# A hybrid decoder block: four pairs of SwiGLU tiles by seven products of quarters

## The chip, the cores and the metric

The kernel runs on one core of one Trainium2 chip. The metric is the device time of one execution in microseconds, median of the runs shown; lower is better.

## The reference, cut to what matters

One decoder block on 512 positions of width 1024, all in float32: two token mixers side by side, merged by gates, then a SwiGLU channel mixer of inner width 2816.

```python
h = rmsnorm(x, norm1_g)
z_glu, z_rx, z_rg, z_ga, z_gb = jnp.split(h @ w_in + b_in, split_idx, axis=-1)

u = z_glu[..., :D_CONV] * jax.nn.sigmoid(z_glu[..., D_CONV:])
u = silu(layernorm(causal_depthwise_conv(u, conv_dw_w, conv_dw_b), ...))
y_a = u @ conv_w_out + conv_b_out

xb = causal_depthwise_conv(z_rx, lru_conv_w, lru_conv_b)
y_b = (rg_lru(xb, ...) * gelu(z_rg)) @ lru_w_out

x = x + (sigmoid(z_ga) * y_a + sigmoid(z_gb) * y_b) @ w_mix_out
h = rmsnorm(x, norm2_g)
x = x + (silu(h @ ffn_w1) * (h @ ffn_w3)) @ ffn_w2
return rmsnorm(x, norm_f_g)
```

The change is in the last matrix products but one, `h @ ffn_w1` and `h @ ffn_w3`: 1024 inputs, 2 x 2816 outputs, 512 positions.

## The kernel before

**Numbers in two parts.** Every float32 operand of a product is split into a high part of TensorE's reduced float32 type (a cast, by ACT) and the low remainder (a subtraction, by DVE or POOL: `split_to`, L106). A product of two split operands is three matmuls: high by high, high by low, low by high (`mm3`, L354). One output tile of 128 columns with 1024 inputs is 8 x 3 = 24 matmuls with 512 positions as the moving side.

**Weights come in chunks.** A chunk is 128x1024 floats, 0.5 MB. `wchunk` (L121) only lists it; `emit_chunk` (L124) issues its load into one of four `raw` buffers (SP's queue), the cast into one of five `hl` buffers, and the subtraction; the `raw` buffer is free when the subtraction has read it, the `hl` buffer when PE has used it. `weights` (L150) emits up to four chunks ahead of the one that is wanted. In the input stage POOL subtracts, from the next stage on DVE.

**Stages in PE's order.** The input stage (`ORDER`, L190; tiles named z, and the gates g) with the depthwise convolution on DVE beside it (`beside`); yb, ya, the mixing product (mxr), the turn of the normalised rows into `h2p` (th), the SwiGLU tiles (f) and the output product (or). The SwiGLU tiles go in pairs k and k + 11, for k = 0 to 10: four products of 24 matmuls, `f1_k`, `f3_k`, `f1_{k+11}`, `f3_{k+11}`. Pair 0 (`first_two`) is done on half a sequence (256 columns) at a time, since the second half of `h2p` comes later.

**Seven products instead of eight.** The mixing and output products already use the Strassen-Winograd scheme: a product of 2 x 2 blocks by seven block products and some sums (`Sevenfold`, L727). Its sums of activations are made in `pair` (L742), its sums of weights in `make_sums` (L265): a load of two blocks into two `raw` buffers, four DVE operations, four stores to DRAM (tiles named ows and ot), from where they are later loaded as chunks. For the output product `make_sums` is called once after each pair of SwiGLU tiles, by `ffn_out` (L875).

**Who sets the order.** Most instructions are put in the order of their engine by a scheduler that works from the order in which they are written and its own estimate of their lengths; each engine then runs its list in order, and SP's list of DMA issues too. `issue_after(ins)` puts a block's instructions of the same engine behind `ins`. Tiles named long, short, raw and hl come from pools with a fixed number of buffers: a new tile waits until an old one is released.

Of the kernel before, what the change touches and what calls it, by code (L numbers as in the profile page):

```python
# [26 lines left out]
ND = D // P  # L27
NR = DR // P
NF = DF // P


SLOTS, SHORT = 69, 5
RAW = 4
HL = 5
AHEAD = 4
# [2 lines left out]
FEW, MANY = 32, 112  # L38

LAG = 12  # L40


ROWS = [
# [32 lines left out]
def tile_block(ctx, tc, a, out):  # L76
    nc = tc.nc
    pool = lambda name, bufs, **k: ctx.enter_context(tc.tile_pool(name=name, bufs=bufs, **k))
    consts = pool("consts", 1)
    raws = pool("raws", RAW)  # L80
    hls = pool("hls", HL)
    psum = pool("psum", 6, space=bass.MemoryType.PSUM)
    psum2 = pool("psum2", 2, space=bass.MemoryType.PSUM)

    def tiles(tag, bufs):
        p_ = pool(tag, bufs)
        return lambda name, dtype=F32: p_.tile([P, T], dtype, tag=tag, name=name)
# [12 lines left out]

    vec, act, pe, pool_e = nc.vector, nc.scalar, nc.tensor, nc.gpsimd

    def sub(eng, o, x, y):
        eng.tensor_tensor(out=o, in0=x, in1=y, op=ALU.subtract)  # L104

    def split_to(h, l, full, eng, copy=act.copy):  # L106

        copy(h, full)  # L108
        sub(eng, l, full, h.bitcast(F32))
# [9 lines left out]
    emitted = [0]  # L119

    def wchunk(key, src, kt, cols, where="hl", lo=pool_e, after=None):  # L121
        chunks.append((key, src, kt, cols, where, lo, after))

    def emit_chunk():  # L124
        key, src, kt, cols, where, lo, after = chunks[emitted[0]]
        emitted[0] += 1
        n = kt * cols
        raw = raws.tile([P, 1024], F32, tag="raw", name=f"raw_{key}")
        rv = raw[:, :n]
        if callable(src):  # L130
            src(raw)
        else:
            nc.sync.dma_start(rv.rearrange("p (k n) -> p k n", k=kt), src)  # L133
# [78 lines left out]
    dram = ctx.enter_context(tc.tile_pool(name="dram", bufs=1, space=bass.MemoryType.DRAM))  # L212
# [70 lines left out]
    ff_order = [j for k in range(NF // 2) for j in (k, k + NF // 2)]  # L283
    for j in ff_order:
        wchunk(f"f1_{j}", w1[:, :, j * P : (j + 1) * P], ND, P, lo=vec)
        wchunk(f"f3_{j}", w3[:, :, j * P : (j + 1) * P], ND, P, lo=vec)
# [67 lines left out]
    def mm3(ps, ws, xs, lo_last=False):  # L354


        n = 3 * len(ws)
        i = 0
        three = [((wh, xh), (wh, xl), (wl, xh)) for (wh, wl), (xh, xl) in zip(ws, xs)]
        if lo_last:  # L360
            three = [q[:2] for q in three] + [q[2:] for q in three]
        for l, r in (q for qs in three for q in qs):
            pe.matmul(ps, l, r, start=i == 0, stop=i == n - 1)  # L363
# [46 lines left out]
    def parts_of(pair_tiles, cs=slice(0, T)):  # L410
        return [(h[:, cs], l[:, cs]) for h, l in pair_tiles]
# [9 lines left out]
    HALVES = [slice(0, 256), slice(256, 512)]  # L421
    EARLY = 2
# [42 lines left out]
    ab, e, s, s2, po, c4 = (sm[:, i, :] for i in range(6))  # L465
# [44 lines left out]
    def beside():  # L510
# [63 lines left out]
    def run_beside(n):  # L574
        for _ in range(n):
            next(side, None)
# [49 lines left out]
    hs = xb  # L626
# [49 lines left out]
    y = []  # L676

    def rg(j):
# [2 lines left out]
        vec.tensor_tensor(out=ps, in0=hs[j], in1=ps, op=ALU.mult)  # L681
        y.append(split(f"y{j}", ps, vec))

    for kind, j in ORDER:
        if kind == "u":
            glu(j)
        elif kind == "rx":
            rx(j)
            run_beside(4)
        elif kind == "g":  # L690
            gates(j)
        elif kind == "r":
            recur(j)
        elif kind == "rg":
            rg(j)
            run_beside(6)
        elif kind == "gb":
            sig(GB, j, sgb, "sgb")
            run_beside(6)
        else:  # L700
            sig(GA, j, sga, "sga")
            run_beside(8)


    for j in range(8):
        ws = w_tiles(f"lo{j}_0", 5) + w_tiles(f"lo{j}_1", 5)
        ps = bank(f"yb{j}")
        mm3(ps, ws, y)
        vec.tensor_tensor(out=sgb[j], in0=ps, in1=sgb[j], op=ALU.mult)
        run_beside(8)  # L710
        if j in (2, 4, 6):
            mixq.make_sums(j // 2 - 1)
    yb = sgb
    run_beside(1000)


    add = lambda o, x, y: vec.tensor_tensor(out=o, in0=x, in1=y, op=ALU.add)
    LO, HI = HALVES
# [8 lines left out]
    class Sevenfold:  # L727
# [28 lines left out]
        def product(self, banks, i, x_, w_, start, stop, again=False):  # L756

            (xh, xl), (wh, wl) = x_, w_
            ts = slice(i * P, (i + 1) * P)
            for n, (l_, r_) in enumerate(((xh, wh), (xh, wl), (xl, wh))):  # L760
                pe.matmul(banks[i], l_[:, ts], r_, start=start and n == 0, stop=stop and n == 2, skip_group_check=again)  # L761
# [66 lines left out]
    h2p = [pairt(f"h2{c}") for c in range(ND)]  # L828
# [42 lines left out]


    o7 = Sevenfold(outq)

    def ffn_out(j, p1, p3):  # L875
        s_ = shortt(f"si{j}")
        act.activation(s_, p1, AF.Silu)
        o7.tile(j, lambda cs, dst: vec.tensor_tensor(out=dst, in0=s_[:, cs], in1=p3[:, cs], op=ALU.mult))  # L878
        if j >= NF // 2:
            with tc.issue_after(turned):  # L880
                outq.make_sums(j - NF // 2)

    first_two = ff_order[:EARLY]
# [13 lines left out]
    for j in ff_order[EARLY:]:  # L897
        p1, p3 = bank(f"f1_{j}"), bank(f"f3_{j}")
        mm3(p1, w_tiles(f"f1_{j}", ND), h2)
        mm3(p3, w_tiles(f"f3_{j}", ND), h2)  # L900
        ffn_out(j, p1, p3)


    x2 = [[longt(f"x2b{t}{h}") for h in range(2)] for t in range(NT)]
# [93 lines left out]
```

## Time and profile before

| | |
|---|---|
| runs | 819.69, 819.13, 818.77 us; median 819.13 |
| profiled execution | 819.27 us, span of its instructions 817.5 us |
| mean granted clock of TensorE | 0.997 |
| PE busy | 805.6 us, 99% |
| DVE busy | 607.6 us, 74% |
| ACT busy | 420.0 us, 51% |
| POOL busy | 149.7 us, 18% |
| moved by DMA | 130.31 MB |

The profile is of one execution. Engines: PE multiplies, PEld loads its weights, DVE, ACT and POOL work on tiles, SP issues DMAs. A row of a group gives line, engine, operation, out<-in by the program's names, shapes and count, then busy time and mean ns of one, then the engine's idle time before them and who ended it. A row of the chain or the timeline begins with its start and length in us. A row of waits reads: engine and line that waited, for whom, us in total, times, longest.

### The profile page before, as it was taken

The numbers are of one execution on the slowest core, as the hardware profiler recorded it, in microseconds if no ns is written. First come the engines' busy times: TensorE is split into PE (matmuls) and PEld (weight loads), VectorE is DVE, ScalarE is ACT, GpSimd is POOL, SyncE is SP. The second block draws the span as 40 slices with busy tenths as digits, with TensorE's granted clock in tenths as the row PEclk, the third lists the DMA queues.
The fourth block names the chain that finished last, engine by engine and source line by source line (L and its number), as shares of the span: only waits on it lengthen the run. The fifth ranks groups of instructions, "written<-read, shape, count | busy, mean of one in ns | idle before, by whom it ended". The sixth has DMA issues, their size and how long they took to land.

```text
span 817.5 us, 10585 instructions
## 1 busy us (share of the span) xinstructions
PE 805.6 (99%) x3750; PEld 673.7 (82%) x3750; DVE 607.6 (74%) x954; ACT 420.0 (51%) x587; POOL 149.7 (18%) x84
## 2 busy tenths in 40 slices
PE   8999999999999999999999999999999999999996
PEld 7988888888888888888888998888888888888885
DVE  4699999999989976876968866455555444688556
ACT  7546688778678565743336543222222222476443
POOL 3564456535534530000000000000000000000000
PEclk9999999999999999999999999999999999999998
DMA  6634433444323412369538448656665666876552
GB/s 207 168 97 117 122 92 102 111 108 112 101 85 110 132 49 67 114 196 292 169 126 248 148 134 267 190 178 204 193 181 187 198 194 205 263 265 205 171 165 103
DMA packets 158343, 130.31 MB, mean 159 GB/s; under 512 B 11367, under 2 KB 128531, under 8 KB 158291
## 3 DMA queue, kind: packets, MB, share of 16 engines
q1 hardware_dynamic: 158291, 129.65, 52.1%
q8 instruction: 29, 0.48, 0.2%
q14 instruction: 23, 0.19, 0.1%
HBM read 108.78 MB, written 17.83 MB: 155 GB/s over the span
## 4 chain that ended last, share of the span: by engine, by line
PE 96%; DMA 1%; SPq 1%; DVE 0%; POOL 0%; ACT 0%; issue 0%
PE z L363 34%; PE f L363 29%; PE or L761 13%; PE yb L363 7%; PE ya L363 5%; PE mxr L761 5%; PE g L643 3%; DMA raw_in<-in_w_in_dram 1%; SPq L319 1%; PE th L403 0%; SPq L312 0%; POOL hl_in L104 0%; DVE of L921 0%; ACT hl_in L108 0%; SPq L133 0%
## 5 line engine op out<-in xcount | busy, mean ns | idle before, releaser
L522 DVE SCALAR_TENSOR_TENSOR cv<-u,par,cv 128x511 f32<-128x511 f32 (+17 forms) x240 | 162.6, 728 | 1.4 <-ACT cv L519 1.2
L104 POOL TENSOR_TENSOR hl_in<-raw_in,hl_in 128x1024 fp32r<-128x1024 f32 x52 | 125.6, 2419 | 136.6 <-ACT hl_in L108 131.8
L108 ACT CAST hl_f<-raw_f 128x1024 fp32r<-128x1024 f32 x44 | 46.2, 1053 | 143.5 <-PE f L363 81.1
L104 DVE TENSOR_TENSOR hl_f<-raw_f,hl_f 128x1024 fp32r<-128x1024 f32 x44 | 53.8, 1222 | 37.4 <-ACT hl_f L108 37.3
L108 ACT CAST hl_in<-raw_in 128x1024 fp32r<-128x1024 f32 x52 | 54.2, 1043 | 11.3 <-PE z L363 7.1
L878 DVE TENSOR_TENSOR ou<-si,f 128x256 f32<-128x256 f32 x22 | 9.3, 422 | 62.2 <-PE f L363 61.6
L108 ACT CAST hl_ob<-raw_ob 128x1024 fp32r<-128x1024 f32 (+1 forms) x23 | 23.4, 1016 | 42.4 <-PE or L761 19.3
L363 PE MATMUL z<-h10h,hl_in 128*128 128x512 f32 (+1 forms) x112 | 42.3, 379 | 1.2 <-DVE h10l L407 0.9
L104 DVE TENSOR_TENSOR hl_ob<-raw_ob,hl_ob 128x1024 fp32r<-128x1024 f32 (+1 forms) x23 | 27.0, 1176 | 19.7 <-ACT hl_ob L108 19.5
L363 PE MATMUL z<-h14h,hl_in 128*128 128x512 f32 (+1 forms) x112 | 41.7, 374 | 0.0
L363 PE MATMUL z<-h13h,hl_in 128*128 128x512 f32 (+1 forms) x112 | 41.7, 374 | 0.0
L363 PE MATMUL z<-h15h,hl_in 128*128 128x512 f32 (+1 forms) x112 | 41.7, 374 | 0.0
L363 PE MATMUL z<-h16h,hl_in 128*128 128x512 f32 (+1 forms) x112 | 41.7, 374 | 0.0
L363 PE MATMUL z<-h11h,hl_in 128*128 128x512 f32 (+1 forms) x112 | 41.7, 374 | 0.0
L363 PE MATMUL z<-h17h,hl_in 128*128 128x512 f32 (+1 forms) x112 | 41.7, 374 | 0.0
L363 PE MATMUL z<-h12h,hl_in 128*128 128x512 f32 (+1 forms) x112 | 41.7, 374 | 0.0
L363 PE MATMUL f<-h22h,hl_f 128*128 128x512 f32 (+1 forms) x96 | 35.4, 371 | 0.0
L363 PE MATMUL f<-h23h,hl_f 128*128 128x512 f32 (+1 forms) x96 | 35.4, 372 | 0.0
L363 PE MATMUL f<-h25h,hl_f 128*128 128x512 f32 (+1 forms) x96 | 35.4, 372 | 0.0
L363 PE MATMUL f<-h24h,hl_f 128*128 128x512 f32 (+1 forms) x96 | 35.4, 371 | 0.0
L363 PE MATMUL f<-h26h,hl_f 128*128 128x512 f32 (+1 forms) x96 | 35.4, 371 | 0.0
L363 PE MATMUL f<-h20h,hl_f 128*128 128x512 f32 (+1 forms) x96 | 35.0, 373 | 0.3 <-ACT h20h L406 0.3
(812 smaller groups left out, 2258.0 us busy)
## 6 DMA issues: line engine op xcount, KB each, us to landing
raw_in<-in_w_in_dram SPq DMA_DIRECT2D x52, 512.0 KB
raw_f<-in_ffn_w_dram SPq DMA_DIRECT2D x44, 512.0 KB
ows<-in_ffn_w_dram SPq DMA_DIRECT2D x22, 512.0 KB
ot<-ows SPq DMA_DIRECT2D x44, 256.0 KB
raw_ob<-in_ffn_w_dram SPq DMA_DIRECT2D x33, 256.0 KB
raw_ot<-ot SPq DMA_DIRECT2D x33, 256.0 KB
raw_lo<-in_lru_w_out_dram SPq DMA_DIRECT2D x16, 320.0 KB
x<-in_x_dram SPq DMA_DIRECT2D x16, 256.0 KB
```

What stands on the lines that cost most here:

```text
L104: eng.tensor_tensor(out=o, in0=x, in1=y, op=ALU.subtract)
L108: copy(h, full)
L319: nc.sync.dma_start(xt[t][h], x_nat[:, t, h * T : (h + 1) * T])
L363: pe.matmul(ps, l, r, start=i == 0, stop=i == n - 1)
L522: vec.scalar_tensor_tensor(out=acc[c][:, s:], in0=u[c][:, : T - s], scalar=dw(c, s), in1=acc[c][:, s:], op0=ALU.mult, op1=ALU.add)
L643: pe.matmul(ps, l, r, start=k == 0, stop=k == len(mms) - 1)
L761: pe.matmul(banks[i], l_[:, ts], r_, start=start and n == 0, stop=stop and n == 2, skip_group_check=again)
L878: o7.tile(j, lambda cs, dst: vec.tensor_tensor(out=dst, in0=s_[:, cs], in1=p3[:, cs], op=ALU.mult))
```

## The change

Pairs 2, 3, 4 and 5 (`SEVEN`) of the SwiGLU tiles are done by seven products of quarters; the other seven pairs stay as they were.

* For such a pair the weight of each of w1 and w3 is cut in 2 x 2 blocks: upper and lower half of the 1024 inputs, columns of tile k and of tile k + 11. The activations are cut in upper and lower half of the inputs and first and second half of the positions. A block product is 4 x 3 matmuls for w1 and as many for w3, of 256 columns, into the two halves of one PSUM bank (`product`): 24 matmuls of 256 columns from one chunk. There are seven, in the order b11, b21, b22, t2, t1, t3, t4. r1 is added to in place by t2 and by t4; ACT copies it out between (`c11`, `q`). Five DVE additions put the results together, four SiLUs of 256 columns and four multiplications follow.
* The four sums of weights t1 to t4 of each of the four pairs are made in the input stage (`make_f_sums`): 16 items, each of four loads of 128x256 (128 KB) into one of two `wsums` buffers, four operations on POOL, placed behind the newest weight subtraction there, and four stores to DRAM; one item every third step of `ORDER`. 64 loads and 64 stores are added to SP's queue there, 64 operations to POOL's. In the SwiGLU stage a sum is loaded as a chunk.
* The sums of activations are made once, behind the turn of `h2p` (`f_inputs`): eight additions on POOL (128x512), sixteen DVE operations of 128x256, eight splits of 128x512 on ACT and DVE.
* `make_sums` for the output product moves from "after each pair" to: two after pair 1, none after pairs 2 and 4, one after 3 and 5, two after each of 6, 7 and 8, the last one after 9 (`out_sums`).
* The long buffers go from 69 to 65, to make room for `wsums`.

In PE's list nothing changes ahead of pair 2. In the lists of ACT and DVE two neighbours are swapped in the input stage; the rest of what differs lies behind pair 0.

```diff
-SLOTS, SHORT = 69, 5
+SLOTS, SHORT = 65, 5
+SEVEN = (2, 3, 4, 5)
+SUMS_AT, SUMS_STEP, SUMS_LAG, STORE_LAG = 4, 3, 2, 5
...
+    wsums = pool("wsums", 2)
...
+    def make_f_sums():
+        todo = [(k, i, c) for k in SEVEN for i in range(2) for c in (0, 2)]
+        sums_due, stores_due = [], []
+        n = 0
+        while todo or sums_due or stores_due:
+            if stores_due and emitted[0] >= stores_due[0][0]:
+                stores_due.pop(0)[1]()
+            if sums_due and n >= sums_due[0][0]:
+                sums_due.pop(0)[1]()
+            if todo and n >= SUMS_AT and (n - SUMS_AT) % SUMS_STEP == 0:
+                k, i, c = todo.pop(0)
+                raw = wsums.tile([P, 1024], F32, tag="wsum", name=f"fws{k}_{i}_{c}")
+                q = [raw[:, 256 * m : 256 * m + 256] for m in range(4)]
+                with tc.issue_after(newest["load"]):
+                    for m, v in zip(("b11", "b12", "b21", "b22"), q):
+                        nc.sync.dma_start(v.rearrange("p (k n) -> p k n", k=2), f_quarter(m, k, (w1, w3)[i], c, c + 2))
+                def sums(q=q, k=k, at=T * i + P * c):
+                    q11, q12, q21, q22 = q
+                    with tc.issue_after(newest["sub"]):
+                        sub(pool_e, q22, q22, q12)
+                        sub(pool_e, q12, q12, q11)
+                        pool_e.tensor_tensor(out=q11, in0=q22, in1=q11, op=ALU.add)
+                        sub(pool_e, q21, q21, q11)
+                    def stores():
+                        with tc.issue_after(newest["load"]):
+                            for m, v in (("t1", q12), ("t2", q11), ("t3", q22), ("t4", q21)):
+                                nc.sync.dma_start(f_sums[m, k][:, at : at + 256], v)
...
     for kind, j in ORDER:
+        next(f_sums_steps, None)
...
-        if j >= NF // 2:
-            with tc.issue_after(turned):
-                outq.make_sums(j - NF // 2)
...
+    def f_inputs():
+        for k in range(4):
+            a1, a2 = [longt(f"hf{c}") for c in (k, k + 4)]
+            for v, c in ((a1, k), (a2, k + 4)):
+                pool_e.tensor_tensor(out=v, in0=h2p[c][0].bitcast(F32), in1=h2p[c][1].bitcast(F32), op=ALU.add)
+            g = [longt(f"hs{k}_{i}") for i in range(2)]
+            s1, s2, s3, s4 = (v[:, cs] for v in g for cs in HALVES)
+            add(s1, a1[:, HI], a2[:, HI])
+            sub(vec, s2, s1, a1[:, LO])
+            sub(vec, s3, a1[:, LO], a1[:, HI])
+            sub(vec, s4, a2[:, LO], s2)
+            s12, s34 = [split(f"hs{k}_{i}", v, vec) for i, v in enumerate(g)]
...
+    def ffn_seven(k):
...
+        product(r1, "a11", "b11")
+        act.copy(c11, r1)
+        product(r2, "a12", "b21")
+        add(c11, r2, c11)
+        out_of(c11, u_[:, LO])
+        product(r3, "s4", "b22")
+        product(r1, "s2", "t2", True)
+        act.copy(q, r1)
+        product(r5, "s1", "t1")
+        add(q, r5, q)
+        add(c12, r3, q)
+        out_of(c12, u_[:, HI])
+        product(r7, "s3", "t3")
+        act.copy(c21, r7)
+        add(q, r7, q)
+        out_of(q, v_[:, HI])
+        product(r1, "a22", "t4", True)
+        add(c21, r1, c21)
+        out_of(c21, v_[:, LO])
+        o7.pair(k, u_, v_)
...
+    for k in range(1, KF):
+        if k in SEVEN:
+            ffn_seven(k)
+            out_sums(k % 2)
+            continue
...
+        out_sums(2 if k < KF - 1 else KF)
```

More of the change, by code (lines that the diff above doesn't have):

```diff
@@ L101, in tile_block @@
     vec, act, pe, pool_e = nc.vector, nc.scalar, nc.tensor, nc.gpsimd
+    newest = {}
     def sub(eng, o, x, y):
-        eng.tensor_tensor(out=o, in0=x, in1=y, op=ALU.subtract)
+        return eng.tensor_tensor(out=o, in0=x, in1=y, op=ALU.subtract)
     def split_to(h, l, full, eng, copy=act.copy):
         copy(h, full)
-        sub(eng, l, full, h.bitcast(F32))
+        last = sub(eng, l, full, h.bitcast(F32))
+        if eng is pool_e:
+            newest["sub"] = last.ins
         return h, l
@@ L132, in emit_chunk @@
         else:
-            nc.sync.dma_start(rv.rearrange("p (k n) -> p k n", k=kt), src)
+            newest["load"] = nc.sync.dma_start(rv.rearrange("p (k n) -> p k n", k=kt), src).ins
         if where == "hl":
@@ L282, in tile_block, with f_quarter @@
     w3 = a["ffn_w3"][0].rearrange("(k p) n -> p k n", p=P)
[L283 to L286, printed above, removed]
+    KF = NF // 2
+    f_sums = {(n, k): dram.tile([P, 1024], F32, tag=f"f{n}_{k}", name=f"f{n}_{k}") for k in SEVEN for n in ("t1", "t2", "t3", "t4")}
+    def f_quarter(n, k, w_, c0, c1):
+        c, j = 4 * (int(n[1]) - 1), k + KF * (int(n[2]) - 1)
+        return w_[:, c + c0 : c + c1, j * P : (j + 1) * P]
@@ new lines, in f_chunk, with load @@
+    def f_chunk(n, k):
+        def load(raw_t):
+            if n[0] == "t":
+                nc.sync.dma_start(raw_t, f_sums[n, k][:, :])
+            else:
+                for i, w_ in enumerate((w1, w3)):
+                    nc.sync.dma_start(raw_t[:, i * T : (i + 1) * T].rearrange("p (k n) -> p k n", k=4), f_quarter(n, k, w_, 0, 4))
+        wchunk(f"f{n}_{k}", load, 8, P, lo=vec)
+    def make_f_sums():
[25 more added lines that the diff above has]
+                                nc.sync.dma_start(f_sums[m, k][:, at : at + 256], v)
+                    stores_due.append((emitted[0] + STORE_LAG, stores))
+                sums_due.append((n + SUMS_LAG, sums))
+            n += 1
+            yield
@@ L287, in tile_block @@
+    for k in range(KF):
+        if k in SEVEN:
+            for n in ("b11", "b21", "b22", "t2", "t1", "t3", "t4"):
+                f_chunk(n, k)
+        else:
+            for j in (k, k + KF):
+                wchunk(f"f1_{j}", w1[:, :, j * P : (j + 1) * P], ND, P, lo=vec)
+                wchunk(f"f3_{j}", w3[:, :, j * P : (j + 1) * P], ND, P, lo=vec)
     outq = Quartered("o", a["ffn_w2"][0].rearrange("(k p) n -> p k n", p=P), NF // 2, vec)
@@ L682, in rg @@
         y.append(split(f"y{j}", ps, vec))
+    f_sums_steps = make_f_sums()
     for kind, j in ORDER:
+        next(f_sums_steps, None)
         if kind == "u":
@@ L710, in tile_block @@
         run_beside(8)
+        next(f_sums_steps, None)
         if j in (2, 4, 6):
@@ L714, in tile_block @@
     run_beside(1000)
+    for _ in f_sums_steps:
+        pass
     add = lambda o, x, y: vec.tensor_tensor(out=o, in0=x, in1=y, op=ALU.add)
@@ L873, in tile_block, with out_sums @@
     o7 = Sevenfold(outq)
+    sums_of = iter(range(KF))
+    def out_sums(n):
+        with tc.issue_after(turned):
+            for _ in range(n):
+                k = next(sums_of, None)
+                if k is not None:
+                    outq.make_sums(k)
     def ffn_out(j, p1, p3):
@@ L878, in ffn_out @@
         o7.tile(j, lambda cs, dst: vec.tensor_tensor(out=dst, in0=s_[:, cs], in1=p3[:, cs], op=ALU.mult))
-        if j >= NF // 2:
-            with tc.issue_after(turned):
-                outq.make_sums(j - NF // 2)
-    first_two = ff_order[:EARLY]
+    first_two = [0, KF]
     wf = [(w_tiles(f"f1_{j}", ND, 0), w_tiles(f"f3_{j}", ND, 0)) for j in first_two]
@@ L896, in tile_block @@
         ffn_out(j, *pf[i])
[L897 to L901, printed above, removed]
+    f_in = {n: [] for n in ("a11", "a12", "a22", "s1", "s2", "s3", "s4")}
+    def f_inputs():
[10 more added lines that the diff above has]
+            s12, s34 = [split(f"hs{k}_{i}", v, vec) for i, v in enumerate(g)]
+            for n, p_, cs in (
+                ("a11", h2p[k], LO), ("a12", h2p[k + 4], LO), ("a22", h2p[k + 4], HI),
+                ("s1", s12, LO), ("s2", s12, HI), ("s3", s34, LO), ("s4", s34, HI),
+            ):
+                f_in[n].append(tuple(v[:, cs] for v in p_))
@@ new lines, in tile_block, with product, out_of @@
+    with tc.issue_after(turned):
+        f_inputs()
+    def ffn_seven(k):
+        u_, v_ = longt(f"ou{k}"), longt(f"ov{k}")
+        def product(ps, x_, w_, again=False):
+            h, l = weights(f"f{w_}_{k}")
+            for i in range(2):
+                for c, (xh, xl) in enumerate(f_in[x_]):
+                    for m, (lw, rx_) in enumerate(((h, xh), (h, xl), (l, xh))):
+                        pe.matmul(
+                            ps[:, HALVES[i]], lw[:, 4 * i + c, :], rx_, start=not (again or i or c or m),
+                            stop=bool(i and c == 3 and m == 2), skip_group_check=True,
+                        )
+        def out_of(c, dst):
+            act.activation(c[:, LO], c[:, LO], AF.Silu)
+            vec.tensor_tensor(out=dst, in0=c[:, LO], in1=c[:, HI], op=ALU.mult)
+        r1, r2, r3, r5, r7 = bank(f"fr1_{k}"), bank2(f"fr2_{k}"), bank(f"fr3_{k}"), bank2(f"fr5_{k}"), bank(f"fr7_{k}")
+        product(r1, "a11", "b11")
+        c11 = shortt(f"c11_{k}")
+        act.copy(c11, r1)
[4 more added lines that the diff above has]
+        product(r1, "s2", "t2", True)
+        q = shortt(f"q_{k}")
+        act.copy(q, r1)
+        product(r5, "s1", "t1")
+        add(q, r5, q)
+        c12 = shortt(f"c12_{k}")
+        add(c12, r3, q)
+        out_of(c12, u_[:, HI])
+        product(r7, "s3", "t3")
+        c21 = shortt(f"c21_{k}")
+        act.copy(c21, r7)
[4 more added lines that the diff above has]
+        out_of(c21, v_[:, LO])
+        o7.uv.append((u_, v_))
+        o7.pair(k, u_, v_)
@@ L904, in tile_block @@
+    for k in range(1, KF):
+        if k in SEVEN:
+            ffn_seven(k)
+            out_sums(k % 2)
+            continue
+        for j in (k, k + KF):
+            p1, p3 = bank(f"f1_{j}"), bank(f"f3_{j}")
+            mm3(p1, w_tiles(f"f1_{j}", ND), h2)
+            mm3(p3, w_tiles(f"f3_{j}", ND), h2)
+            ffn_out(j, p1, p3)
+        out_sums(2 if k < KF - 1 else KF)
     x2 = [[longt(f"x2b{t}{h}") for h in range(2)] for t in range(NT)]
```

## The prediction

> **What bounds the kernel now.** I read the head of the page first, then the chain that ended last, then who waited on PE, then stretches of time.
>
> ```profile
> span 817.5 us, 10585 instructions
> PE 805.6 (99%) x3750; PEld 673.7 (82%) x3750; DVE 607.6 (74%) x954; ACT 420.0 (51%) x587; POOL 149.7 (18%) x84
> PE 96%; DMA 1%; SPq 1%; DVE 0%; POOL 0%; ACT 0%; issue 0%
> GB/s 207 168 97 117 122 92 102 111 108 112 101 85 110 132 49 67 114 196 292 169 126 248 148 134 267 190 178 204 193 181 187 198 194 205 263 265 205 171 165 103
> ```
> The end is set by PE: 96% of the chain. The pieces of the chain give what PE pays for one matmul.
>
> ```profile
> 72.14 1.85 PE g L643 x8
> ...
> 246.68 65.30 PE z L363 x288
> ...
> 461.61 11.51 PE f L363 x96
> ...
> 478.61 226.43 PE f L363 x1033
> 705.04 102.97 PE or L761 x453
> ```
> A product of 512 columns costs 65.30 / 288 = 226.7 ns. The 96 matmuls of 11.51 us are the first SwiGLU tiles on half a sequence, 256 columns: 119.9 ns each. So a half costs 13 ns more than half of a whole. Pairs 1 to 10 of SwiGLU tiles end where the "or" products begin, at 705.04; pair 2, the first that is changed, starts nine pairs earlier (below: 21.76 us each), at 509.2.
>
> PE hardly ever waits (all waits of over a few tenths are in the first 27 us):
>
> ```profile
> PE z L363 <- POOL hl_in L104: 0.3, 1, 0.3
> PE f L363 <- ACT h20h L406: 0.3, 1, 0.3
> ```
>
> Stretches (busy us of PE, PEld, DVE, ACT, POOL, then clock, DMA share, GB/s): the input stage, the first halves, pairs 1 and 2, and four later pairs.
>
> ```profile
> 28.00:280.00 252.00, 252.00 (x1156) 210.32 (x1155) 243.20 (x382) 178.53 (x221) 127.01 (x70) 1.00 0.38 105
> 461.00:484.00 23.00, 22.66 (x184) 21.95 (x182) 14.56 (x29) 12.74 (x25) 0.00 (x0) 1.00 0.29 93
> 484.00:528.00 44.00, 44.00 (x210) 37.05 (x209) 27.84 (x42) 13.83 (x19) 0.00 (x0) 1.00 0.76 239
> 528.00:616.00 88.00, 88.00 (x390) 72.89 (x389) 45.42 (x72) 24.10 (x32) 0.00 (x0) 1.00 0.62 192
> ```
> DVE is nearly full in the input stage (243.2 of 252 us) and half empty beside the SwiGLU pairs; POOL works in the input stage alone.
>
> **PE's part of the change.** A pair of tiles is four products of 24 matmuls of 512 columns: 96 x 226.7 ns = 21.76 us. With seven products of quarters it is 7 x 24 = 168 matmuls of 256 columns: 168 x 119.9 ns = 20.14 us. That is 12.5% less arithmetic, but only 1.62 us a pair, since the 13 ns are paid 168 times. Four pairs: 6.5 us, all on the path.
>
> [...]
>
> Could loading weights hold the short matmuls back? In the stretch 461:484, 182 loads took 21.95 us, 121 ns each, beside matmuls of that size; a load fits. I take nothing for it.
>
> **The vector engines beside the pairs.** Rows of DVE, ACT, and POOL (mean ns of one after the comma):
>
> ```profile
> L104 DVE TENSOR_TENSOR hl_f<-raw_f,hl_f 128x1024 fp32r<-128x1024 f32 x28 | 34.2, 1221 | 27.1 <-ACT hl_f L108 27.1
> L104 DVE TENSOR_TENSOR ows<-ows,ows 128x512 f32<-128x512 f32 x16 | 11.0, 688 | 0.3
> L878 DVE TENSOR_TENSOR ou<-si,f 128x256 f32<-128x256 f32 x16 | 6.8, 422 | 50.8 <-PE f L363 50.8
> ```
> ```profile
> L108 ACT CAST hl_f<-raw_f 128x1024 fp32r<-128x1024 f32 x28 | 29.5, 1054 | 110.1 <-PE f L363 65.1 <-issue 45.1
> L877 ACT ACTIVATE si<-f 128x512 f32<-128x512 f32 x16 | 9.4, 588 | 0.0
> L108 ACT CAST os1p<-os 128x256 fp32r<-128x256 f32 x8 | 3.2, 400 | 0.0
> ```
> ```profile
> L104 POOL TENSOR_TENSOR hl_in<-raw_in,hl_in 128x1024 fp32r<-128x1024 f32 x52 | 125.6, 2419 | 136.6 <-ACT hl_in L108 131.8 <-PE g L643 2.9 <-DMA raw_gate<-in_lru_wa_dram 1.4
> L104 POOL TENSOR_TENSOR hl_gate<-raw_gate,hl_gate 128x512 fp32r<-128x512 f32 x10 | 13.4, 1340 | 14.1 <-ACT hl_gate L108 9.8 <-DMA raw_gate<-in_lru_wx_dram 4.2
> L104 POOL TENSOR_TENSOR hl_gate<-raw_gate,hl_gate 32x256 fp32r<-32x256 f32 x6 | 4.9, 820 | 0.5
> ```
> A changed pair asks of DVE: seven chunk subtractions, 7 x 1.22 = 8.5; five additions from PSUM, by the 512-wide row 5 x 0.69 = 3.4; four multiplications, 4 x 0.42 = 1.7; the pair's own sums and split, 0.69 + 5 x 0.42 = 2.8; half a set of the sums for the last weights, 2 x 0.69 = 1.4. That is 17.8 of 20.14 us. ACT: 7 x 1.05 + 3 copies of 0.59 + 4 x 0.40 + 1.0 = 11.7 us. Both fit, DVE with 2.3 us to spare, so in the steady state I charge nothing. What hides it is the ring of five split weights: a chunk's buffer is free four products ahead of its use.
>
> ```profile
> 499.49 1.23 DVE L104 TENSOR_TENSOR hl_f<-raw_f,hl_f 128x1024 fp32r<-128x1024 f32 x1 [0.31 <-ACT hl_f L108]
> ```
> ```profile
> 519.92 0.39 PE L363 MATMUL f<-h20h,hl_f 128*128 128x512 f32 x1
> ```
> This chunk is ready 19.2 us before PE takes it; with products of 24 x 119.9 ns = 2.88 us the ring reaches only 4 x 2.88 = 11.5 us ahead, and cast and subtraction take 2.3 of that.
>
> The entrance is the tight place. The sums of the activations are built once, between 479.6 and the third product of pair 2 (509.2 + 5.8 = 515.0): DVE 16 x 0.42 + 8 x 0.69 = 12.2 us, POOL 8 x 1.34 = 10.7 us, ACT 8 x 0.59 = 4.7 us. Add to the 27.84 us that DVE works in 484:528 these 12.2, three more chunks 3.7, five additions 3.4, and take off one set of sums that now comes later, 2.8: 44.3 of 44 us. So DVE falls behind there, and the order of its queue decides. In the changed order of DVE the first addition of pair 1's sums stands ahead of the last activation split, and it waits for a load into a buffer that the stores of pair 0's sums must leave first. The t4 chunk's load waits likewise for the stores of pair 1's sums, and on SP the loads of pair 3 are queued behind it. Rows of a load and its landing, and of waits for stores:
>
> ```profile
> 482.57 3.22 SPq L133 DMA_DIRECT2D raw_f<-in_ffn_w_dram  x2
> ...
> 490.50 0.32 SPq L278 DMA_DIRECT2D ot<-ows  x1
> ```
> ```profile
> 486.90 1.05 ACT L108 CAST hl_f<-raw_f 128x1024 fp32r<-128x1024 f32 x1 [1.38 <-DMA raw_f<-in_ffn_w_dram]
> ```
> ```profile
> SPq L133 <- DMA ot<-ows: 23.0, 11, 3.2
> SPq L133 <- POOL hl_in L104: 130.7, 37, 9.5
> ```
> A load lands 486.90 - 482.57 = 4.3 us after its issue, a store is waited for 23.0 / 11 = 2.1 us. Counting DVE's list by hand with these durations: pair 0's sums are stored at 503.1, so pair 1's second load goes out at 505.5 and lands at 510; the last activation split ends at 511.3, tile 12's outputs at 512.7, ten steps of pair 1 and its sums take 5.6, t1's own subtraction 1.2: 519.5. PE wants t1 at 509.2 + 4 x 2.88 = 520.7. The store that t4's buffer waits for goes out at 516.2 and lands at 518.5, t4's load at 522.9, cast and subtraction end at 525.2, and PE wants it at 509.2 + 6 x 2.88 = 526.5. Margins of 1.2 and 1.3 us on some forty steps: the stall is 0 at best and 3 us at worst; I take 1.0, nearer the lower end, because both margins are positive.
>
> **DMA.** A pair moved 4 chunks of 0.52 MB and 2.1 MB of sums, 4.2 MB in 21.76 us (the 192 GB/s of 528:616). A changed pair moves 7 x 0.52 + 1.05 = 4.7 MB in 20.14 us, 234 GB/s; pairs 6 to 8, which now make two sets of sums each, 6.3 MB, 289 GB/s. The page's best slice moved 292. It fits without room, but those pairs enter with a full ring (19 us) and can lose 2 us each: nothing charged, 3 us at worst.
>
> **The input stage.** 16 items of four subtractions or additions of 128x256 on POOL; the nearest row is 820 ns (and 1340 - 256 x 2.1 = 800): 64 x 0.81 = 52 us. POOL goes from 127 to 179 of 252 us. Queued behind each item's 3.3 us is the next chunk's subtraction. Pairing POOL's subtractions in order with PE's runs of 24, the tightest is
>
> ```profile
> 253.18 2.40 POOL L104 TENSOR_TENSOR hl_in<-raw_in,hl_in 128x1024 fp32r<-128x1024 f32 x1 [4.56 <-ACT hl_in L108]
> ```
> ```profile
> 262.86 0.39 PE L363 MATMUL z<-h10h,hl_in 128*128 128x512 f32 x1
> ```
> ready 7.3 us early, over twice an item. SP's queue gets 128 more issues (0.32 us in the row of 490.50, 41 us); it waits 130.7 us for POOL's buffers already, so it has the time. If an item's 3.3 us, a store's 2.1 and a new load's 4.3 all fell on that chunk, PE would wait 3.3 + 2.1 + 4.3 - 7.3 = 2.4 us. DVE loses only where POOL holds it up:
>
> ```profile
> 110.81 2.40 POOL L104 TENSOR_TENSOR hl_in<-raw_in,hl_in 128x1024 fp32r<-128x1024 f32 x1 [4.23 <-ACT hl_in L108]
> ```
> ```profile
> 111.50 2.26 DVE L104 TENSOR_TENSOR xb4l<-xb,xb4h 128x512 fp32r<-128x512 f32 x1
> ```
> A 512-wide DVE subtraction of two SBUF tiles took 2.26 us instead of 0.69, to the end of POOL's instruction. Ten such splits, each held up by one more 0.81 us at most: 8 us. The earliest has the least in hand,
>
> ```profile
> 53.80 0.69 DVE L104 TENSOR_TENSOR xb0l<-xb,xb0h 128x512 fp32r<-128x512 f32 x1
> ```
> ready at 54.5 for the "g" products of 72.14. Nothing charged; 2.4 us at worst.
>
> The four fewer long buffers (65 for 69) make the split of pair 9 wait for the last SwiGLU matmuls; it is needed 37 us later (nine steps of 18 matmuls). Nothing.
>
> **Sum.** 819.27 (the profiled execution, 817.5 of span) - 6.5 + 1.0 = 813.8; the median of the runs is 0.14 lower: 813.6.
>
> **Rivals.** *No stall at all*: 812.6, chance 0.24. For it: PE now waits for nothing. *A late chunk in every changed pair*: stores of the sums and chunks share four buffers and one queue, so the t-chunk behind them comes 1.5 us late each time; 819.1 - 6.5 + 6 = 818.6. It decides if loads take over 6 us at 234 GB/s. Chance 0.14. *POOL's lock at the entrance*: none of POOL's 10.7 us hidden, DVE reaches the third chunk of pair 2 at 507 instead of 499, and 6.6 us of stall cancel the gain: 819.2, chance 0.06. [...] Against the price: POOL starts at 478 and DVE must wait for the ring until 499 anyway. *The input stage stalls* by its 2.4 us: 816.0, chance 0.04. *DVE sets the pace of the changed pairs*, the slower case: its rows above show 50.8 + 27.1 us of idle waits in eight pairs, 9.7 a pair; if half of that stays in the order of its queue, a pair takes 17.8 + 4.9 = 22.7 us, 2.6 more than PE, four pairs 10.4: 819.1 - 6.5 + 10.4 = 823.0. It decides once DVE waits over 2.3 us a pair. Against it: 97% busy in the input stage shows that it can run without waits. Chance 0.11. The forecast keeps 0.41.
>
> **The numbers.** A difference of 0.2%, 1.6 us, is about what can be told here. Faster takes the forecast, the case without stall, the input stage and half of the late chunks: 0.76. Same is the other half and the lock, 0.13; slower is DVE's pace, 0.11. The range runs from below the case without stall, 811.8, to above the late chunks and the lock, 820.0.
>
> **What would show it.** Right: "fr" matmuls 119.9 ns apart, pairs 2 to 5 at 20.1 us, PE waiting 1 us or so in pair 2 for an hl_ft chunk, and PE's run of z as long as now. Wrong: PE waiting in each of pairs 2 to 5 for DVE (pace) or ACT behind raw_ft (late chunk), PE waits for POOL before 312 us, or a spacing of the "fr" matmuls well over 120 ns.

## The result, and the profile after

| | before | after |
|---|---|---|
| runs, one chip | 819.69, 819.13, 818.77, 818.67; median 818.95 us | 816.61, 814.38, 813.68, 813.84; median 814.11 us |
| ratio | | 0.9946, 95% interval 0.9924 to 0.9967 |
| profiled execution, span | 819.27, 817.5 us | 816.61, 814.8 us |

The change is 4.8 us faster; 813.6 was forecast. The profiled execution is the slowest of the four, which matters below: it shows one cost at 4.1 us that a second profile of the same kernel shows at 2.5. The head of the page after and its GpSimd row in the slices:

```profile
span 814.8 us, 11572 instructions
PE 801.8 (98%) x4038; PEld 683.9 (84%) x4038; DVE 648.0 (80%) x1010; ACT 445.2 (55%) x627; POOL 210.2 (26%) x156
POOL 3565778758665740000000042000000000000000
```
288 more matmuls in less PE time (801.8 us for 805.6), since 672 of them are half as wide. The chain in order of time shows two things:

```profile
161.31 15.12 PE z L437 x67
176.43 6.70 issue
...
206.24 29.08 PE z L437 x120
...
327.46 6.80 PE yb L437 x30
...
513.33 80.63 PE fr L1016 x672
593.96 108.83 PE f L437 x480
702.79 102.93 PE or L840 x453
```
First, the four changed pairs take 80.63 us without a gap, 120.0 ns a matmul, 20.16 us a pair, and the five unchanged pairs behind them 226.7 ns a matmul. Second, the chain, which before the change was PE from end to end here, leaves PE at 176 us and comes back only at 206; yb begins at 327.46. Before the change it began at

```profile
323.34 6.80 PE yb L363 x30
```
on the same origin (the first split, xb0l, starts at 53.8 us in both traces). So 4.1 us are lost in the input stage, and 6.4 are won in the pairs: "or" starts at 702.79 instead of 705.04. Who waited on PE from 150 to 320 us, where the trace before has no PE wait at all:

```profile
PE z L437 <- DVE xb L741: 1.2, 1, 1.2
PE g L717 <- DVE th L731: 0.6, 1, 0.6
```
PE waits for VectorE, not for GpSimd. The table of stretches, before and after (PE, PEld, DVE, ACT, POOL, granted clock, DMA share, GB/s):

```profile
186.00:206.50 20.50, 20.50 (x92) 16.95 (x91) 20.27 (x31) 17.87 (x22) 11.16 (x7) 1.00 0.45 122
206.00:210.00 4.00, 4.00 (x20) 3.30 (x19) 4.00 (x8) 3.22 (x5) 1.49 (x2) 1.00 0.46 131
```
```profile
186.00:206.50 20.50, 18.66 (x81) 14.69 (x80) 19.65 (x28) 17.25 (x21) 16.84 (x15) 0.99 0.63 182
206.00:210.00 4.00, 3.76 (x10) 3.03 (x11) 4.00 (x7) 3.48 (x4) 1.43 (x2) 0.57 0.43 118
```
PE is idle for 1.84 us (20.50 - 18.66) while VectorE does 28 instructions in the time of 31, and behind the wait the clock is granted at 0.57: 10 matmuls in 4 us instead of 20. The timeline has this as two matmuls that wait, and then a spacing of 0.43 us instead of 0.227:

```profile
203.82 0.50 PE L717 MATMUL g<-xb7h,hl_gate 128*128 128x512 f32 x1 [0.63 <-DVE th L731]
206.24 0.77 PE L437 MATMUL z<-h10h,hl_in 128*128 128x512 f32 x1 [1.22 <-DVE xb L741]
207.23 0.63 PE L437 MATMUL z<-h10h,hl_in 128*128 128x512 f32 x1
207.66 0.63 PE L437 MATMUL z<-h11h,hl_in 128*128 128x512 f32 x1
```
Taking every spacing of PE from 202 to 210 us less 0.227, the waits and the first matmuls behind them make 2.4 us, the slow clock 1.7: together the 4.1.

Why VectorE is late stands 13 us earlier. GpSimd's list and VectorE's split, after:

```profile
186.78 0.74 POOL L113 TENSOR_TENSOR fws<-fws 128x256 f32<-128x256 f32 x1
187.59 0.73 POOL L113 TENSOR_TENSOR hl_gate<-raw_gate,hl_gate 32x256 fp32r<-32x256 f32 x1
...
190.03 0.74 POOL L113 TENSOR_TENSOR fws<-fws 128x256 f32<-128x256 f32 x1
190.72 2.40 POOL L113 TENSOR_TENSOR hl_in<-raw_in,hl_in 128x1024 fp32r<-128x1024 f32 x1
```
```profile
190.91 2.76 DVE L113 TENSOR_TENSOR xb8l<-xb,xb8h 128x512 fp32r<-128x512 f32 x1
```
and before:

```profile
187.60 2.41 POOL L104 TENSOR_TENSOR hl_in<-raw_in,hl_in 128x1024 fp32r<-128x1024 f32 x1 [0.52 <-ACT hl_in L108]
```
```profile
189.73 0.83 DVE L104 TENSOR_TENSOR xb8l<-xb,xb8h 128x512 fp32r<-128x512 f32 x1
```
An item of the sums (fws) pushes the chunk's subtraction from 187.60 to 190.72, and so onto the split of xb8, which then ends 0.55 us behind GpSimd's instruction: at 193.67 instead of 190.56. VectorE has 20.27 us of work in 20.5 there; of 3.1 us lost it had 1.3 in hand, and PE waits for the rest. Of the 3.1 us, 1.9 is the split's own length and 1.2 its later start (190.91 for 189.73), since VectorE's cast of hl_gate ahead of it had to wait for GpSimd longer (0.82 us for 0.45) and itself took 0.81 us for 0.28. That is a reading so far; the runs decide.

### The profile page after: what moved, and what is told of

Read it like the earlier page. It is cut to its first block, busy times and chain, and to the rows that moved or that the text cites. A ratio compares the mean times of both kernels' runs of the same rounds, so it can differ in the third digit from the quotient of the medians.

```text
span 814.8 us, 11572 instructions
## 1 busy us (share of the span) xinstructions
PE 801.8 (98%) x4038; PEld 683.9 (84%) x4038; DVE 648.0 (80%) x1010; ACT 445.2 (55%) x627; POOL 210.2 (26%) x156
## 4 chain that ended last, share of the span: by engine, by line
PE 92%; DVE 3%; DMA 1%; issue 1%; SPq 1%; POOL 0%; ACT 0%; POOLq 0%
PE z L437 31%; PE f L437 19%; PE or L840 13%; PE fr L1016 10%; PE yb L437 7%; PE ya L437 5%; PE mxr L840 5%; PE g L717 2%; DMA raw_in<-in_w_in_dram 1%; DVE cv L596 1%; SPq L393 1%; PE th L477 0%; DVE xb8l L113 0%; SPq L386 0%; POOL hl_in L113 0%
## 5 line engine op out<-in xcount | busy, mean ns | idle before, releaser
L117 ACT CAST hl_f<-raw_f 128x1024 fp32r<-128x1024 f32 x28 | 29.3, 1051 | 51.4 <-DMA raw_f<-in_ffn_w_dram 37.7
L113 DVE TENSOR_TENSOR hl_f<-raw_f,hl_f 128x1024 fp32r<-128x1024 f32 x28 | 36.3, 1308 | 16.4 <-ACT hl_f L117 16.4
L113 DVE TENSOR_TENSOR hl_ob<-raw_ob,hl_ob 128x1024 fp32r<-128x1024 f32 (+1 forms) x23 | 27.1, 1177 | 20.3 <-ACT hl_ob L117 20.2
L113 POOL TENSOR_TENSOR fws<-fws 128x256 f32<-128x256 f32 x48 | 36.3, 756 | 2.4
L113 DVE TENSOR_TENSOR ows<-ows,ows 128x512 f32<-128x512 f32 x22 | 15.2, 690 | 19.8 <-DMA ows<-in_ffn_w_dram 19.7
L113 DVE TENSOR_TENSOR hl_ot<-raw_ot,hl_ot 128x1024 fp32r<-128x1024 f32 (+1 forms) x17 | 20.1, 1191 | 11.8 <-ACT hl_ot L117 11.4
L117 ACT CAST hl_ot<-raw_ot 128x1024 fp32r<-128x1024 f32 (+1 forms) x17 | 17.5, 1028 | 17.2 <-PE or L840 15.5
L437 PEld LDWEIGHTS z<-h10h,hl_in 128*128 128x128 f32 x112 | 21.4, 191 | 6.3 <-ACT g L723 1.6
L437 PEld LDWEIGHTS z<-h11h,hl_in 128*128 128x128 f32 x112 | 21.4, 191 | 3.9
```

The source lines that it names most:

```text
L113: return eng.tensor_tensor(out=o, in0=x, in1=y, op=ALU.subtract)
```

## The experiments

Each was timed beside the kernel before; the ratio is to that. Three theories of the input stage's loss: **the hold-up** (GpSimd's operations make VectorE's longer and later; the expectations call it the lock), **transfers** (the items' loads and stores delay the stage's chunks), **chance** (the profiled execution happened to be late).

| run | median us | before | ratio, 95% interval |
|---|---|---|---|
| the change again | 813.88 | 818.87 | 0.9941 (0.9930 to 0.9953) |
| no sums | 811.65 | 818.41 | 0.9921 (0.9907 to 0.9934) |
| transfers only | 811.94 | 818.41 | 0.9921 (0.9908 to 0.9935) |
| GpSimd only | 813.94 | 818.41 | 0.9946 (0.9933 to 0.9960) |
| sums only, on the kernel before | 821.92 | 818.41 | 1.0044 (1.0031 to 1.0056) |
| tenth item moved | 811.63 | 818.91 | 0.9910 (0.9896 to 0.9925) |
| sixth item moved | 814.67 | 818.87 | 0.9950 (0.9938 to 0.9962) |
| late sums | 821.80 | 818.91 | 1.0030 (1.0019 to 1.0041) |
| late sums, six pairs | 859.40 | 818.91 | 1.0495 (1.0478 to 1.0512) |
| five pairs | 812.53 | 818.87 | 0.9929 (0.9914 to 0.9945) |
| six pairs | 817.04 | 818.87 | 0.9978 (0.9963 to 0.9994) |
| five pairs, sums earlier | 810.53 | 818.68 | 0.9896 (0.9878 to 0.9913) |

**No sums.** The t-chunks read other rows, nothing is made in the input stage.

```diff
-nc.sync.dma_start(raw_t, f_sums[n, k][:, :])
+nc.sync.dma_start(raw_t, a["ffn_w2"][0].rearrange("(k p) n -> p k n", p=P)[:, 4 * (k - 2) + int(n[1]) - 1, :])
-f_sums_steps = make_f_sums()
+f_sums_steps = iter(())
```


> Leaves out the weights' sums altogether: no loads, no GpSimd operations and no stores of them in the input stage; the t-chunks of the four pairs are filled with rows of another weight, the same 0.52 MB each. The changed pairs are untouched. Lock theory (GpSimd's 64 operations hold up VectorE's operations between SBUF tiles, VectorE falls behind by 206 us, PE waits and its clock dips) and transfer theory (the 16 items' loads and stores delay the chunks of the stage) both expect 818.95 - 6.5 = 812.5 us, the first yb product at 323.3 us as before the change, the ten xb-l subtractions at 12.0 us in all. Chance theory (the late yb of the profiled run is no work of the change) expects 814.1 as the change itself. With PE 1.6 to 4.1 us earlier at the entrance of the changed pairs, a stall there of up to 1 us may show; if it does, 813.5.

811.65: 6.76 us less than before, where 6.5 had been worked out for the pairs. No PE wait from 150 to 320 us, xb8l 0.83 us. The pairs' gain is as computed, and the entrance, which PE now reaches earlier, has no stall either.

**Sums only, on the kernel before.** `make_f_sums` with its buffers and calls is added to the kernel before; the pairs stay.

```diff
+f_sums_steps = make_f_sums()
 for kind, j in ORDER:
+    next(f_sums_steps, None)
 ...
```


> The kernel before, with the weights' sums made and stored in the input stage as in the change and used by nobody; the pairs stay as before. Lock and transfer theories expect the input stage's loss alone: 818.95 + 1.6 = 820.6 us by the medians (814.11 against 812.5), up to 823.1 if it is as in the profiled run, with PE waiting for VectorE near 203 to 207 us. Chance theory expects 819.0.

821.92, 3.5 us more than before, with the same two waits of 1.2 and 0.6 us and the slow clock behind them (0.64 in 206:210). The loss belongs to the sums, and the chance theory falls. Its five times lie within 1 us of each other, so this kernel seems to pay for the slow clock every time; one profile alone cannot show that.

**Transfers only.** The four GpSimd operations of an item are left out.

```diff
-sub(pool_e, q22, q22, q12)
-sub(pool_e, q12, q12, q11)
-pool_e.tensor_tensor(out=q11, in0=q22, in1=q11, op=ALU.add)
-sub(pool_e, q21, q21, q11)
```


> The change without the four GpSimd operations of each item: loads and stores stay, so the t-chunks hold quarters that were not added. Lock theory expects 812.5 us, xb-l subtractions at 12.0 us in all as before, no wait of PE between 28 and 323 us. Transfer theory expects 814.1 or more, yb at 325 to 327.5 us.

811.94, as without sums. The 17 MB that the items load and store (16 items of 0.52 MB each way) cost nothing that can be told. In the row of this run the stretch moves 195 GB/s, PE is busy all its 20.50 us, and xb8l takes 0.82 us:

```profile
186.00:206.50 20.50, 20.50 (x92) 16.95 (x91) 20.47 (x32) 17.87 (x22) 10.90 (x6) 1.00 0.68 195
```
The transfer theory falls.

**GpSimd only.** The operations at the same steps, on two zeroed tiles, no loads and stores.

```diff
-raw = wsums.tile([P, 1024], F32, tag="wsum", ...)
+raw = idle[len(todo) % 2]
...
-with tc.issue_after(newest["load"]):
-    for m, v in zip(("b11", "b12", "b21", "b22"), q):
-        nc.sync.dma_start(v.rearrange("p (k n) -> p k n", k=2), f_quarter(m, k, (w1, w3)[i], c, c + 2))
...
-stores_due.append((emitted[0] + STORE_LAG, stores))
```


> The change with the 64 GpSimd operations at the same steps of the emission, but on two tiles that were set to zero once: no loads and no stores of sums; the t-chunks are filled with rows of another weight. Lock theory expects 814.1 us or more (up to 816.6), xb-l subtractions at about 14.4 us in all and a PE wait for VectorE around 203 to 207 us with the granted clock near 0.55 for some 3 us behind it. Transfer theory expects 812.5.

813.94, and the split and the stretches of this run:

```profile
189.62 2.75 DVE L113 TENSOR_TENSOR xb8l<-xb,xb8h 128x512 fp32r<-128x512 f32 x1
```
```profile
186.00:206.50 20.50, 18.64 (x81) 14.67 (x80) 20.47 (x29) 17.22 (x22) 16.08 (x14) 1.00 0.43 118
206.00:210.00 4.00, 4.00 (x19) 3.31 (x18) 4.00 (x7) 2.20 (x3) 1.72 (x1) 1.00 0.48 135
```
The same 1.86 us of idle PE, to a tenth, but the clock stays at 1.00: by the medians this run pays 2.3 us against the run without sums. In the traces, counted from the first split (xb0l) to the first yb product, it is 272.0 us here, 269.5 without sums as in the kernel before, and 273.6 in the profiled execution of the change: 2.5 us lost, or 4.1 with the slow clock. GpSimd's operations alone bring the loss back, with xb8l ending 0.54 us behind the subtraction that GpSimd began at 189.44 us and worked on for 2.39; one expectation missed: here no dip of the clock followed the waits.

**The tenth item moved, the sixth item moved.** Does every item cost a little, or this one everything?

```diff
-SUMS_AT, SUMS_STEP, SUMS_LAG, STORE_LAG = 4, 3, 2, 5
+SUMS_STEPS, SUMS_LAG, STORE_LAG = [n for n in range(4, 53, 3) if n != 31], 2, 5
-if todo and n >= SUMS_AT and (n - SUMS_AT) % SUMS_STEP == 0:
+if todo and n in SUMS_STEPS:
```
(The second run has 19 in the place of 31.)

> The change with one of its 16 items moved: the tenth (GpSimd at 186.8 to 190.8 us, which pushes the 2.40 us subtraction behind it onto VectorE's xb8-l split at 190.9 us) goes behind the last one. Local theory (the loss is this one collision at a place where VectorE has no slack: xb8-l 2.76 us instead of 0.83): xb8-l back near 0.83 us, PE's waits of 1.2 and 0.6 us gone or under 0.3 us, 811.9 us against 818.4 before, a ratio of 0.992. Spread theory (every item costs its share, wherever it stands): 15 items cost what 16 cost, 813.8, a ratio of 0.9945.

> The change with another one of its 16 items moved behind the last: the sixth, which GpSimd does at 134.5 to 137.7 us, where it meets no split of xb. Local theory: xb8-l stays at 2.76 us, PE's waits of 1.2 and 0.6 us stay, the time is the change's, a ratio of 0.9946 (814 us). Spread theory (GpSimd has less to do ahead of 206 us, whichever item goes): the waits go as they did when the tenth item was moved, 811.7 us, a ratio of 0.991.

With the tenth item moved behind the last: 811.63: all 64 operations are still done in the input stage, and nothing is lost there. GpSimd and VectorE of that run:

```profile
186.45 2.41 POOL L113 TENSOR_TENSOR hl_in<-raw_in,hl_in 128x1024 fp32r<-128x1024 f32 x1 [0.94 <-ACT hl_in L117]
```
```profile
188.91 0.68 DVE L113 TENSOR_TENSOR xb8l<-xb,xb8h 128x512 fp32r<-128x512 f32 x1
```
The subtraction is over at 188.86, and the split begins at 188.91. With the sixth item moved instead: 814.67, xb8l at 2.77 us, the two waits as they were. The loss is one collision at a place where VectorE has almost nothing in hand, not a tax on every operation.

**The change again**, beside these runs.

> The change itself once more, beside the other kernels of this set on one chip. From the runs so far a ratio of 0.9946 to before: 814 us against 818.5; PE's waits of 1.2 and 0.6 us near 203 to 207 us are there again, with or without a dip of the clock behind them (2.3 or 4.1 us in all).

813.88, the two waits, no dip of the clock in its profile, and 272.0 us from the first split to yb. Against the run with the tenth item moved the intervals of the ratios do not overlap.

**Late sums.** All items at the end of the input stage and in the two stages behind it (yb and ya), where VectorE has more idle time (in the profile after the change it is busy 38.66 us of 327 to 378, and 33.55 of 382 to 426).

```diff
+SUMS_STEPS, SUMS_LAG, STORE_LAG = [n for n in range(55, 78) if n % 3 != 0], 1, 1
 ...
 for n, j in enumerate(mixq.order()):
 ...
+    next(f_sums_steps, None)
```


> The change with all 16 items moved to the end of the input stage and the two stages behind it (the steps from about 280 us on, yb and ya), two items in three steps, where VectorE is busy 77 to 78% and GpSimd hardly at all. Lock theory: no wait of PE in the input stage, 812.0 us against 818.4 before, a ratio of 0.992. A rival for this kernel: 1 MB of loads and stores per item on top of the 68 to 134 GB/s there, and locks on VectorE's chunk subtractions in yb and ya, make chunks late: PE waits in yb or ya by 1 to 3 us, 813 to 815.

821.80 (the profiled execution is the fastest, 818.69): slower than the kernel before. The rival had late chunks, but PE's waits a stage too early and too small a price. PE waits neither in the input stage nor in yb or ya, but at the first mixing products. The stretches of ya and of the mixing product, of this run and (second fence) of the run with the tenth item moved:

```profile
378.00:422.00 44.00, 44.00 (x196) 36.44 (x195) 38.14 (x56) 13.32 (x18) 16.25 (x21) 1.00 0.92 279
422.00:460.00 38.00, 34.11 (x140) 27.28 (x139) 33.55 (x47) 20.27 (x30) 3.63 (x4) 0.91 0.88 281
```
```profile
378.00:422.00 44.00, 44.00 (x195) 36.42 (x195) 34.16 (x59) 14.51 (x20) 0.00 (x0) 1.00 0.56 179
422.00:460.00 38.00, 38.00 (x177) 31.65 (x176) 31.32 (x53) 21.22 (x38) 0.00 (x0) 1.00 0.67 208
```
The DMA engines are busy 92% instead of 56%; ACT waits for loads, and PE at the first mixing products for VectorE:

```profile
ACT hl_co L117 <- DMA raw_co<-in_conv_w_out_dram: 24.5, 6, 6.3
PE mxr L838 <- DVE sga L895: 3.9, 2, 2.7
```
The transfers are not alone in this. In ya VectorE needs 38.14 us for 56 instructions where it needed 34.16 for 59, while GpSimd works 16.25 us beside it where it worked 0. One row of each run, 378 to 428 us, VectorE's sums for the mixing product:

```profile
L113 DVE TENSOR_TENSOR mxe<-mxu,mxv 128x256 f32<-128x256 f32 x6 | 4.0, 670 | 0.1
```
```profile
L113 DVE TENSOR_TENSOR mxe<-mxu,mxv 128x256 f32<-128x256 f32 x8 | 3.4, 423 | 0.1
```
Late loads and longer VectorE operations both stand in this trace, and no run separates them.

**Late sums, six pairs.** 24 items, one in each step, `SEVEN = (2, 3, 4, 5, 6, 7)`.

> As the run with late sums, but six pairs (2 to 7) from seven products, 24 items, one in each step. Lock theory with 1.62 us a pair: 6 x 1.62 = 9.7 us less than before, 808.7 + 0.3 = 809.0, a ratio of 0.9885. Rival: one item a step (1 MB in 5.4 to 6.8 us, 154 to 193 GB/s beside the stage's own 68 to 134) is too much for the transfers or for VectorE; PE waits in yb and ya, and the time is that of four pairs or above, 812 to 815.

859.40: the same with half as much again to move. PE's waits are spread over yb, ya and the mixing product, the largest

```profile
PE mxr L838 <- ACT hl_mxb L117: 13.3, 4, 7.8
```
The free engines of those stages were no room. In the run with four pairs the DMA engines were 92% busy beside the late sums, and VectorE's sums for the mixing product took 670 ns instead of 423; how much each cost was not tried.

**Five and six pairs** at the change's own pace of one item in three steps, without the tenth's place; the last items go into yb and ya.

```diff
-SEVEN = (2, 3, 4, 5)
+SEVEN = (2, 3, 4, 5, 6)            # or (2, 3, 4, 5, 6, 7)
+SUMS_STEPS, SUMS_LAG, STORE_LAG = [n for n in range(4, 65, 3) if n != 31], 2, 5   # or 77 for 65
 ...
-            out_sums(k % 2)
+            out_sums(1 if k > 3 else k % 2)      # six pairs only
```


> Five pairs (2 to 6) from seven products: 20 items at every third step as in the change, the place of the tenth left out, so that the items reach into the two stages behind the input stage (1 MB in 18 us, 58 GB/s there). With 1.62 us a pair and no loss in the input stage 811.6 - 1.6 = 810.0 us, a ratio of 0.989. Rival: the pairs that make two sums of the output weights each are one fewer, and transfers at 260 to 290 GB/s there come late: 811 to 814.

> Six pairs (2 to 7) from seven products: 24 items at every third step without the tenth's place, and the sums of the output weights one in each pair from 4 to 7 (so that pairs 8 and 9 make two each as before). With 1.62 us a pair 811.6 - 3.2 = 808.4 us, a ratio of 0.987. Rival: VectorE at 17.8 + 1.4 = 19.2 us of 20.14 a pair, or the transfers (5.2 MB in 20.14 us, 260 GB/s), fall behind in pairs 4 to 7, or the or products at the end get their chunks late as in the run with late sums and six pairs (waits of 2.7, 2.3 and 1.9 us there): 811 to 816.

Five pairs: 812.53, no better than four, with one new wait at the output product, and VectorE's wait that stands before it:

```profile
PE or L838 <- DVE ov L967: 1.2, 1, 1.2
```
```profile
DVE ows L113 <- DMA ows<-in_ffn_w_dram: 3.7, 1, 3.7
```
A set of sums of the output weights, pushed into pair 10, has its load late. Six pairs: 817.04, spread over 813.75 to 821.18; the input stage has no wait, but the output product has one of 2.9 us for ACT, and the changed pairs have these:

```profile
PE fr L1017 <- ACT q L1036: 2.7, 2, 1.7
PE fr L1017 <- ACT c L1029: 1.7, 2, 0.9
PE fr L1017 <- DVE hl_ft L113: 1.2, 1, 1.2
ACT hl_ft L117 <- DMA raw_ft<-ft: 14.3, 8, 4.0
```
ACT copies a product's bank (q, c) in a list with casts that wait for their loads (the last row, of 509 to 640 us; in the change the same wait is 3.7 us in all, from 509 to 594); that the loads are what is too much there was not tried by itself.

**Five pairs, sums earlier.** One set of the output weights' sums goes from pair 10 into pair 6.

```diff
-            out_sums(k % 2)
+            out_sums(k % 2 + (k == 6))
```


> Five pairs as in the last run of five pairs, with one set of the output weights' sums taken out of pair 10, where VectorE waited 3.7 us for its load and PE 1.2 us for VectorE behind it at the first or product, and put into pair 6. If that wait was all that stood between 812.5 and four pairs' 811.6 less 1.6: 810.0 us, a ratio of 0.989, and no wait of PE at the or products. Rival: pair 6 gets late chunks in its place, and the time stays at 811.6 to 813.

810.53, the lowest median of all, and no PE wait at the output product. In the traces pairs 2 to 10 take 187.86 us, 1.60 less than the 189.46 of four pairs. By the medians the kernel is 8.15 us faster than before, against 7.28 for four pairs with the tenth item moved, and the intervals of these two ratios overlap: that a fifth pair shortens the whole by its 1.6 us is likely, not shown.

## Why the prediction was right or wrong

**The pairs: right.** 6.5 us were worked out; the run without sums has 6.76, the one with transfers only 6.47, each to its own kernel before. The spacing is 120.0 ns. One sentence of the working is off: a half costs 119.9 - 113.35 = 6.6 ns more than half of a whole, and the 13 ns are what two halves cost more, paid 84 times a pair. The sum used the measured lengths and is not touched.

**DVE's pace, late chunks, DMA in the later pairs: rightly charged with nothing.** No wait of PE from pair 2 to the output product, and VectorE works 16.7 us of the 20.2 of a changed pair, where 17.8 were counted.

**The entrance: 1.0 us was charged, 0 was paid.** The margins were nearly as counted by hand, both positive, and a stall was charged all the same for the forty steps of the count. For t4 of pair 2 (margin 1.3 by hand) and the first chunk of pair 3, the subtractions and the matmuls that use them:

```profile
527.48 1.23 DVE L113 TENSOR_TENSOR hl_ft<-raw_ft,hl_ft 128x1024 fp32r<-128x1024 f32 x1 [2.12 <-ACT hl_ft L117]
530.91 1.23 DVE L113 TENSOR_TENSOR hl_fb<-raw_fb,hl_fb 128x1024 fp32r<-128x1024 f32 x1 [2.21 <-ACT hl_fb L117]
```
```profile
530.44 0.28 PE L1016 MATMUL fr<-h24h,hl_ft 128*128 128x256 f32 x1
533.32 0.28 PE L1016 MATMUL fr<-h20h,hl_fb 128*128 128x256 f32 x1
```
They are ready 1.73 and 1.18 us early, the latter the tightest of all 28 chunks. PE comes there 4.1 us late in this execution, but in the run without sums, where it does not, t4's margin is much the same, 1.9 us.

**The input stage: nothing was charged, 2.3 us are paid by the medians, 2.5 in the traces without the slow clock and 4.1 in the profiled execution. This is the step that failed.** The prediction saw the hold-up (xb4l at 2.26 us instead of 0.69, to the end of GpSimd's instruction) and even bounded it, ten splits "held up by one more 0.81 us at most: 8 us", then let it go because the earliest split had 17 us in hand. Two things were wrong. The size: an item does not hold the split up by its own 0.74 us, it moves the 2.40 us subtraction behind it onto the split, 1.93 us at once, on top of a start that is 1.2 us later. And the margin: it was read at the first split, at 54 us, while the margin that counts is VectorE's own list where that has almost no idle time, 20.27 us of work in 20.5. The chunks, whose lead was watched instead, stayed as early as they were: the tightest of the stage is done at 265.24 and used at 272.42.

```profile
262.83 2.41 POOL L113 TENSOR_TENSOR hl_in<-raw_in,hl_in 128x1024 fp32r<-128x1024 f32 x1
```
```profile
272.42 0.39 PE L437 MATMUL z<-h10h,hl_in 128*128 128x512 f32 x1
```
"PE waits for POOL before 312 us" was named as the sign of failure; the sign that came was PE waiting for VectorE. Of the signs of being right, the spacing and the pairs' time came; the wait in pair 2 and a run of z as long as before did not. The rival for this stage had 2.4 us for another reason, a late chunk, and is not borne out.

**The total** of 813.6 against 814.11 is good partly by luck, since two errors cancel: 1.0 too much at the entrance, 2.3 too little in the input stage. The terms as measured, 818.95 - 6.5 + 2.3, give 814.8; what is left is within the spread of the four runs.

## What to carry to other kernels

Work given to an idle engine is not free because the engine is idle: look at whether the busiest one's instructions grow longer beside that work (here a split of 0.83 us took 2.76), and at where it moves the instructions that were already in its list. A margin has to be read for the engine that has none left, in the stretch where it is busy all the time, not for the data that one happens to watch. And where such a loss is a single collision, moving one piece of work by some steps can win back all of it (here 2.3 of the 6.8 us that the pairs bring), while moving all the work to stages with more idle time on the engines cost 10 us, where late loads and longer VectorE operations met and were not told apart.

## What the runs showed of the hardware

- VectorE's split of a 128x512 tile (a subtraction of two SBUF tiles), where it started beside a GpSimd subtraction of 2.40 us, ended half a microsecond behind it: xb4l before the change at 113.76 us for 113.21, xb8l before at 190.56 for 190.01, xb8l after at 193.67 for 193.12. xb8l took 2.76 us when it started 0.19 us after the subtraction, 0.83 us when 0.28 us of that was left, and 0.68 us when it started 0.05 us behind its end (tenth item moved). With the 17 MB of transfers and without GpSimd's operations of the sums it took 0.82 us, and that run 811.94 us, against 0.83 and 811.65 without both.
- The two waits of PE, 1.84 to 1.86 us of idle PE, cost 2.5 us (272.0 from the first split to yb, for 269.5), and 4.1 us in the profiled execution of the change, where the granted clock fell to 0.57 behind them. In five profiles with the same two waits (the change, the change again, GpSimd only, sums only, sixth item moved) it fell in two, to 0.57 and 0.64 in the stretch from 206 to 210 us, and was 1.00 in three (in the profile of the change again over 200 to 210). In the profile of the change the matmuls from 206.80 to 209.36 us stand 0.42 to 0.43 us apart instead of 0.227, and the loss is 1.6 us more; the change and the change again are one kernel, with the drop in one and not in the other. What decides between the two was not shown.
